# The order of wide and narrow products of two neighbouring weight blocks in a two-layer decoder trunk

## The chip, the core and the metric

The kernel runs on one core of a Trainium2 chip. The metric is the device time of one execution in microseconds (us); the median of three runs of the kernel before is 844.6 us (844.43 to 845.07). A core has several engines that run side by side and wait for one another by semaphores: TensorE (PE in the profile; its weight loads are the row PEld), VectorE (DVE), ScalarE (ACT), GpSimd (POOL) and SyncE (SP, which here only starts transfers).

## The reference

The input x has 256 positions of 2048 features, in float32. Two layers follow one another, each a normalisation, one wide input projection, an attention, a gate, an output projection and a residual addition; a last normalisation ends it.

```python
for i in range(DEPTH):                       # DEPTH = 2
    h = rmsnorm(x, norm_g[i])
    if i % 2 == 0:                           # forgetting attention, 32 heads x 64
        p = h @ fox_w_in[j]                  # q, k, v, gate (2048 each), 32 forget logits
        y = fox_attention(q, k, v, log_f)
        w_out = fox_w_out[j]
    else:                                    # window of 128, 32 query and 4 key heads, sinks, partial rope
        p = h @ swa_w_in[j]                  # q, k, v, gate
        y = swa_attention(q, k, v, swa_sinks[j])
        w_out = swa_w_out[j]
    y = y * silu(gate)
    x = x + y @ w_out
return rmsnorm(x, final_g)
```

Nearly all the arithmetic lies in `h @ w_in` and `y @ w_out`.

## The kernel before, in words

**One product in float32 precision from two halves.** Weights and activations are each split into a high part (rounded to the type fp32r) and a low part (the remainder). ScalarE makes the high half of a weight block (line 210), VectorE the low one (line 211); both lie side by side in a tile `w`. The split activations lie in `xs` (for the input projections) and `ys` (for the output projections). A product needs high times high, high times low and low times high. With `halves` set, the first two are one matmul with a moving operand of 512 columns, whose two halves of 256 columns go to two halves of one PSUM bank: this is called a *wide* product here. The third is a matmul of 256 columns, a *narrow* product. Each matmul is preceded by a load of its stationary operand.

**Units, parts and blocks.** A `Unit` is 256 output features over all 16 slices (`KT`) of the contracted dimension. It is loaded in parts, nearly all of four slices (s = 4). A part is multiplied twice: `block(u, p, 0)` and `block(u, p, 1)` (c = 0 and c = 1) give the two halves of 128 output rows, in two PSUM banks. A block is four wide products and then four narrow ones. After the last part's block, `unit.consume(c, ps)` reads the finished bank: it scales, rotates or splits queries and keys, applies the gate, or adds to the residual. The first unit of layer 1 (`v0`, parts of 1, 2 or 3 slices, 288 columns) and the very last unit have `halves=False`: there all products are 256 or 288 columns wide.

**The order of the work.** `stream` is the list of all parts. The main loop at the end walks over it. For each part it issues the loads of the part three further on (`fetch`), then block c = 0 of this part, then block c = 1 of the part before (`prev`). So a part's weights are used in two steps of the loop. One step is called a *pair* below: two blocks, 16 products. Matmuls keep program order (`mm`, line 73); other instructions are put into order by the framework's planner.

**Ticks.** Each block calls `tick()` after every second product, so four times with s = 4, and eight times a pair. `after(n, fn)` puts work n ticks later. `consume` of c = 0 starts a group's attention: `self.attend(kt, due, ...)` registers scores (PE), transposes (PE), and the product with the values (PE) at fixed numbers of ticks from there. The lists for these ticks are `FOX_DUE`, `FOX_FIRST`, `FOX_LAST`, `SWA_DUE` and `SWA_LAST`:

```python
FOX_DUE = ((16, 34), (40, 60), 106)   # (scores, transposes) of head pairs 0 and 1; values
SWA_DUE = ((16, 40), (44, 64), 74)
```

Between scores and transposes of a pair of heads lies a chain on VectorE and ScalarE: bias and row maximum (line 299), exponentials (line 309), division (line 320). The second normalisation's sums are asked for 10 ticks after the last block of the first layer has been consumed (`after(10, norm)` in `to_layer1`). PSUM is filled with four banks for units (`ps_acc`), two for scores (`ps_s`) and two for transposes and values (`ps_t`). The weight tiles `w` have five buffers.

Of the kernel before, what the change touches and what calls it, by code (L numbers as in the profile page):

```python
# [51 lines left out]
def trunk(  # L52
# [19 lines left out]
    def mm(*args, **kw):  # L72
        tc.keep_in_program_order(nc.tensor.matmul(*args, **kw))  # L73
# [31 lines left out]
    def after(steps, fn):  # L105
        due.setdefault(clock[0] + max(steps, 1), []).append(fn)

    def tick():
        clock[0] += 1
        for fn in due.pop(clock[0], ()):  # L110
            with tc.high_priority(HP):
                fn()
# [103 lines left out]
    def block(unit, p, c):  # L216
        _, _, _, kt0, s = unit.parts[p]
        w, a = loaded[unit, p], unit.acts
        if p == 0:
            pool, tag = unit.acc  # L220
            unit.ps[c] = pool.tile([P, 512], F32, tag=tag, name="acc")
        n = unit.n if unit.kind == "tok" else S
        both, ps = unit.ps[c], unit.ps[c][:, 0:n]
        cs = slice(c * P, (c + 1) * P)
        def operands(i):

            kt = kt0 + i
            if unit.kind == "tok":
                return a[:, kt, 0, cs], a[:, kt, 1, cs], w[:, i]
            return w[:, i, 0, cs], w[:, i, 1, cs], a[:, kt]  # L230

        first, last = kt0 == 0, kt0 + s == KT
        ops = [operands(i) for i in range(s)]
        if unit.halves:

            for i, (sh, _, mv) in enumerate(ops):
                mm(both, sh, mv.rearrange("p h n -> p (h n)"), start=first and i == 0, stop=False)
                if i % 2:
                    tick()
            if s % 2:  # L240
                tick()
            for i, (_, sl, mv) in enumerate(ops):
                mm(ps, sl, mv[:, 0, :], start=False, stop=last and i == s - 1)
                if i % 2:
                    tick()
        else:
            for i, (sh, sl, mv) in enumerate(ops):
                mm(ps, sh, mv[:, 0, :], start=first and i == 0, stop=False)
                mm(ps, sh, mv[:, 1, :], start=False, stop=False)
                mm(ps, sl, mv[:, 0, :], start=False, stop=last and i == s - 1)  # L250
                tick()
        if p == len(unit.parts) - 1:
            unit.consume(c, unit.ps[c])

    def low_half(ps):
        s = work.tile([P, S], F32, tag="row", name="half", bufs=4)
# [292 lines left out]
    def out_units(src, done):  # L549
        def consumer(u):  # L550
            def consume(c, ps):
                m = 2 * u + c
                nc.vector.tensor_add(xT[:, m, :], low_half(ps), xT[:, m, :])
                nc.vector.tensor_add(xT[:, m, :], ps[:, 0:S], xT[:, m, :])
                done(m)

            return consume

        first = [
            Unit(  # L560
                [(src[u, 0], [4, 4]), (src[u, 1][:, 0:4, :], [4]), (src[u, 1][:, 4:8, :], [4])],
                "wgt", consumer(u), acts=ys,
            )
            for u in range(2)
        ]
        return first + [whole(src[u], "wgt", consumer(u), acts=ys) for u in range(2, 8)]
# [195 lines left out]
    last_out = out_units(swa_out_d, to_end)  # L762
# [44 lines left out]
    start = [(u, p) for p in range(3) for u in (v0, q0, k0)]  # L807
# [6 lines left out]
    def fetch(upto):  # L814
        while fetched[0] < min(upto, len(stream)):
            load(*stream[fetched[0]])
            fetched[0] += 1
# [20 lines left out]
    sink = cpool.tile([P, H], F32, name="sink")  # L838
    after(SINK, lambda: nc.gpsimd.dma_start(out=sink, in_=sink_d.partition_broadcast(P)))

    prev = None
    for i, (u, p) in enumerate(stream):
        fetch(i + 1 + LOOK)
        if u is last_out[7]:
            if p == 0:
                block(*prev, 1)
            block(u, p, 0)
            continue
        block(u, p, 0)
        if prev is not None:  # L850
            block(*prev, 1)
        prev = (u, p)
    for p in range(len(last_out[7].parts)):
        block(last_out[7], p, 1)


# ---- launch: one core; the host only lays arrays out
# [62 lines left out]
```

## Time and profile before

| what | value |
|---|---|
| median of three runs | 844.6 us |
| the profiled execution's own time | 844.48 us |
| its span, first to last instruction | 842.7 us |
| PE busy | 830.0 us (98%), 4972 matmuls |
| PE weight loads busy | 720.9 us (86%) |
| VectorE busy | 656.7 us (78%) |
| ScalarE busy | 542.6 us (64%) |
| granted TensorE clock, mean | 0.997 |

The page gives the busy time of each engine, the groups of instructions that cost most, and the chain of work that ended last. A matmul's own duration in these rows (395 ns for 512 columns, 281 to 283 ns for 256) holds its passage through the array, and neighbouring matmuls overlap in it. So what a matmul costs is read from the distance between the starts of two matmuls that follow one another, and an engine that is called busy isn't thereby shown to be at its peak.

### The profile page before, as it was taken

To read this page: it belongs to the slowest core of one execution; us is meant where nothing else is said; L and a number is where in the kernel's file an instruction comes from. 1 tells how busy PE (TensorE), PEld (TensorE's weight loads), DVE (VectorE), ACT (ScalarE), POOL (GpSimd) and SP (SyncE) were. 2 spreads that over 40 slices of the span, in tenths; PEclk is the share of its full clock that TensorE was granted. 3 is DMA by queue.
4 is the path that set the end of the run, shared out by engine and by line. 5 is a ranking of instruction groups with operands and counts; after the bars stand their busy time and mean duration, and the time that the engine had idled before them with its cause. 6 is when DMAs were issued, how large, how long until landed. Compare 5 with 4: busy or idle time off the path is not lost.

```text
span 842.7 us, 13456 instructions
## 1 busy us (share of the span) xinstructions
PE 830.0 (98%) x4972; PEld 720.9 (86%) x4972; DVE 656.7 (78%) x1380; ACT 542.6 (64%) x1061; POOL 67.8 (8%) x93
## 2 busy tenths in 40 slices
PE   8999999999999999999999999999999999999995
PEld 7888888888888888888888888888888888888885
DVE  6898868678686877867677778788898889877555
ACT  7678757667575765746555555567766776666562
POOL 1022001101010010100011110000000000003210
PEclk9999999999999999999999999999999999999998
DMA  8765555555465555554465554544444535364523
GB/s 300 258 218 214 188 187 171 186 192 189 159 227 161 171 209 166 196 177 154 160 211 192 198 195 158 188 159 139 161 150 151 164 137 174 126 203 163 191 100 101
DMA packets 27969, 150.51 MB, mean 179 GB/s; under 512 B 3152, under 2 KB 8176, under 8 KB 12288
## 3 DMA queue, kind: packets, MB, share of 16 engines
q1 hardware_dynamic: 24176, 141.94, 48.9%
q0 software_dynamic: 1408, 6.36, 2.4%
q10 hardware_dynamic: 2320, 1.35, 0.5%
q8 instruction: 39, 0.64, 0.3%
q14 instruction: 26, 0.21, 0.1%
HBM read 147.50 MB, written 2.15 MB: 178 GB/s over the span
## 4 chain that ended last, share of the span: by engine, by line
PE 94%; DVE 4%; ACT 1%; issue 1%; DMA 0%; ACTq 0%; DVEq 0%
PE acc L73 85%; PE ps_s L73 3%; PE psy L73 3%; PE pt L76 2%; DVE w L211 1%; ACT w L210 1%; DMA wraw<-in_vf_dram 0%; DVE st L299 0%; DVE xs L159 0%; DVE xT L667 0%; DVE ssq L784 0%; ACT st L309 0%; DVE q L330 0%; PE ps_n L73 0%; DVE st L320 0%
## 5 line engine op out<-in xcount | busy, mean ns | idle before, releaser
L73 PE MATMUL acc<-xs,w 128*128 128x512 f32 (+1 forms) x2624 | 483.2, 339 | 0.2 <-DVE w L211 0.2
L73 PEld LDWEIGHTS acc<-xs,w 128*128 128x128 f32 x2624 | 405.2, 189 | 59.9 <-issue 3.9
L211 DVE TENSOR_TENSOR w<-wraw,w 128x1024 fp32r<-128x1024 f32 (+3 forms) x271 | 325.1, 1204 | 108.1 <-ACT w L210 106.1
L210 ACT CAST w<-wraw 128x1024 fp32r<-128x1024 f32 (+3 forms) x271 | 277.3, 1028 | 133.3 <-PE acc L73 124.2
L73 PE MATMUL acc<-ys,w 128*128 128x512 f32 x960 | 170.8, 338 | 0.0
L73 PEld LDWEIGHTS acc<-ys,w 128*128 128x128 f32 x960 | 147.4, 189 | 21.5 <-issue 0.6
L73 PE MATMUL acc<-w,xs 128*128 128x256 f32 (+2 forms) x608 | 114.3, 335 | 2.5 <-DVE w L211 1.3
L73 PEld LDWEIGHTS acc<-w,xs 128*128 128x128 f32 x608 | 93.8, 189 | 14.6 <-DVE w L211 2.0
L257 ACT COPY half<-acc 128x256 f32<-128x256 f32 x112 | 41.2, 368 | 60.2 <-PE acc L73 59.3
L309 ACT ACTIVATE st<-st,mx 128x128 f32<-128x128 f32 (+1 forms) x128 | 56.6, 444 | 13.3 <-DVE mx L509 7.9
L576 POOL TENSOR_TENSOR acc<-acc,sq 128x256 f32<-128x256 f32 x28 | 29.9, 1069 | 105.2 <-ACT sq L570 105.2
L363 ACT COPY pts<-pt 128x384 f32<-128x384 f32 x64 | 30.4, 475 | 11.1 <-PE pt L76 11.1
L73 PE MATMUL ps_s<-kk,q 128*128 128x128 f32 (+1 forms) x256 | 35.7, 281 | 0.2
L320 DVE TENSOR_SCALAR st<-st,rl 128x128 f32<-128x128 f32 (+1 forms) x128 | 32.9, 320 | 1.1
L73 PEld LDWEIGHTS ps_s<-kk,q 128*128 128x128 f32 x256 | 32.1, 190 | 1.3 <-issue 0.4
L76 PE MATMUL pt<-ident,st 128*128 128x128 f32 x192 | 31.5, 273 | 0.0
L574 POOL COPY acc<-sq 128x256 f32<-128x256 f32 x2 | 1.9, 936 | 334.0 <-ACT sq L570 334.0
L125 POOL TENSOR_SCALAR_AFFINE_SELECT bc<-bc 128x256 f32<-128x256 f32 x32 | 22.9, 737 | 56.7 <-DMA bc<-negc_d 56.7
L494 POOL DMA_DIRECT2D bc<-negc_d x16 | 8.9, 555 | 214.9 <-DVE mx L508 176.7
L76 PEld LDWEIGHTS pt<-ident,st 128*128 128x128 f32 x192 | 23.2, 140 | 2.3
L159 DVE SCALAR_TENSOR_TENSOR xs<-xT,g_sb,xs 128x256 fp32r<-128x256 f32 x32 | 22.0, 712 | 3.8 <-ACT xs L158 3.8
L329 ACT CAST q<-qT 64x256 fp32r<-64x256 f32 x32 | 12.8, 401 | 18.6 <-DVE qT L697 18.2
(132 smaller groups left out, 578.4 us busy)
## 6 DMA issues: line engine op xcount, KB each, us to landing
wraw<-in_fox_in_dram SPq DMA_DIRECT2D x58, 1024.0 KB, 4.9
wraw<-in_swa_in_dram SPq DMA_DIRECT2D x36, 1024.0 KB, 4.9
wraw<-in_fox_out_dram SPq DMA_DIRECT2D x14, 1024.0 KB, 4.9
wraw<-in_swa_out_dram SPq DMA_DIRECT2D x14, 1024.0 KB, 4.9
bc<-negc_d POOLq DMA_DIRECT2D x16, 384.0 KB, 4.3
wraw<-in_fox_in_dram SPq DMA_DIRECT2D x6, 512.0 KB, 4.5
wraw<-in_fox_out_dram SPq DMA_DIRECT2D x4, 512.0 KB, 3.7
wraw<-in_swa_out_dram SPq DMA_DIRECT2D x4, 512.0 KB, 3.7
```

The source lines that it names most:

```text
L73: tc.keep_in_program_order(nc.tensor.matmul(*args, **kw))
L76: tc.keep_in_program_order(nc.tensor.transpose(out, in_, ident))
L125: nc.gpsimd.affine_select(out=ap, in_=ap, compare_op=ALU.is_ge, fill=NEG, base=base, pattern=pattern, channel_multiplier=mult,)
L159: nc.vector.scalar_tensor_tensor(out=xs[:, kt, 1, :], in0=xT[:, kt, :], scalar=g, in1=xs[:, kt, 0, :].bitcast(F32), op0=ALU.mult, op1=ALU. ...
L210: nc.scalar.copy(w[:, :, 0, :], raw)
L211: nc.vector.tensor_tensor(out=w[:, :, 1, :], in0=raw, in1=w[:, :, 0, :].bitcast(F32), op=ALU.subtract)
L257: nc.scalar.copy(s, ps[:, S : 2 * S])
L309: nc.scalar.activation(st[:, hh, rng], st[:, hh, rng], AF.Exp, bias=nm[:, qb, hh : hh + 1], accum_out=l[:, qb, hh : hh + 1],)
L320: nc.vector.tensor_scalar_mul(st[:, hh, rng], st[:, hh, rng], rl[:, qb, hh : hh + 1])
L329: nc.scalar.copy(q2[w, hh, :], t[w, :])
L363: nc.scalar.copy(group.pts[hh][:, self.j, :], pt[:, 0 : 3 * P])
L576: nc.gpsimd.tensor_add(sums[0], sums[0], s)
```

## The change

`block` no longer issues the narrow products of a block with `halves` itself: it issues the wide ones and returns a function, `narrow`, that issues the narrow ones and then calls `consume` where the part is the unit's last. The main loop calls block c = 0 of the new part (wide products only), then all of block c = 1 of the part before, wide and narrow, and then the new part's narrow products. A block without `halves` is issued whole as before, and what it returns does nothing. In the very last unit the order stays.

The order on PE in one step of the loop was, with four slices: 4 wide (new part, c = 0), 4 narrow (same), 4 wide (part before, c = 1), 4 narrow (same). It becomes: 4 wide (new part), 4 wide (part before), 4 narrow (part before), 4 narrow (new part). The eight ticks of the step move with the products.

```diff
+        def done():
+            if p == len(unit.parts) - 1:
+                unit.consume(c, unit.ps[c])
+
+        def narrow():
+            for i, (_, sl, mv) in enumerate(ops):
+                mm(ps, sl, mv[:, 0, :], start=False, stop=last and i == s - 1)
+                if i % 2:
+                    tick()
+            done()
+
         if unit.halves:
 
             for i, (sh, _, mv) in enumerate(ops):
@@
             if s % 2:
                 tick()
-            for i, (_, sl, mv) in enumerate(ops):
-                mm(ps, sl, mv[:, 0, :], start=False, stop=last and i == s - 1)
-                if i % 2:
-                    tick()
-        else:
-            for i, (sh, sl, mv) in enumerate(ops):
...
-        if p == len(unit.parts) - 1:
-            unit.consume(c, unit.ps[c])
+            return narrow
+        for i, (sh, sl, mv) in enumerate(ops):
...
+        done()
+        return lambda: None
@@
     for i, (u, p) in enumerate(stream):
         fetch(i + 1 + LOOK)
         if u is last_out[7]:
             if p == 0:
-                block(*prev, 1)
-            block(u, p, 0)
+                block(*prev, 1)()
+            block(u, p, 0)()
             continue
-        block(u, p, 0)
+        narrow = block(u, p, 0)
         if prev is not None:
-            block(*prev, 1)
+            block(*prev, 1)()
+        narrow()
         prev = (u, p)
     for p in range(len(last_out[7].parts)):
-        block(last_out[7], p, 1)
+        block(last_out[7], p, 1)()
```

More of the change, by code (lines that the diff above doesn't have):

```diff
@@ L241, in block @@
                 tick()
-            for i, (_, sl, mv) in enumerate(ops):
-                mm(ps, sl, mv[:, 0, :], start=False, stop=last and i == s - 1)
-                if i % 2:
-                    tick()
-        else:
-            for i, (sh, sl, mv) in enumerate(ops):
[L248 to L251, printed above, removed]
-        if p == len(unit.parts) - 1:
-            unit.consume(c, unit.ps[c])
+            return narrow
+        for i, (sh, sl, mv) in enumerate(ops):
+            mm(ps, sh, mv[:, 0, :], start=first and i == 0, stop=False)
+            mm(ps, sh, mv[:, 1, :], start=False, stop=False)
+            mm(ps, sl, mv[:, 0, :], start=False, stop=last and i == s - 1)
+            tick()
+        done()
+        return lambda: None
     def low_half(ps):
```

## The prediction

> **What bounds the kernel now.** I read the head of the page first, then who waited for whom, then the matmuls by form, then single starts in the timeline.
>
> ```profile
> span 842.7 us, 13456 instructions
> ...
> PE 830.0 (98%) x4972; PEld 720.9 (86%) x4972; DVE 656.7 (78%) x1380; ACT 542.6 (64%) x1061; POOL 67.8 (8%) x93
> ...
> PEclk9999999999999999999999999999999999999998
> ```
>
> ```profile
> ACT w L210 <- PE acc L73: 124.2, 110, 2.6
> ...
> PE rows L73 <- DVE tail L655: 2.5, 1, 2.5
> ...
> PE acc L73 <- DVE w L211: 1.4, 3, 0.9
> PE acc L73 <- ACT w L210: 1.1, 2, 0.8
> ```
>
> The second view has total, times and longest, in us. PE waits 2.5 us for weights in all and 2.5 us at the end; ScalarE's weight copies wait 124.2 us for PE to give buffers back. So weights are ahead of PE, and PE's own pace sets the time. The clock is full. A change to the order on PE can act in three ways only: the pace of products, a new wait on PE, or an old wait that goes.
>
> ```profile
> L73 PE MATMUL acc<-xs,w 128*128 128x512 f32 x1312 | 360.7, 395 | 0.0
> L73 PE MATMUL acc<-xs,w 128*128 128x256 f32 x1312 | 212.6, 283 | 0.2 <-DVE w L211 0.2
> L73 PE MATMUL acc<-ys,w 128*128 128x512 f32 x480 | 131.8, 395 | 0.0
> L73 PE MATMUL acc<-ys,w 128*128 128x256 f32 x480 | 76.5, 281 | 0.0
> L73 PE MATMUL acc<-w,xs 128*128 128x512 f32 x256 | 71.0, 399 | 0.0
> L73 PE MATMUL acc<-w,xs 128*128 128x256 f32 x256 | 41.2, 282 | 0.0
> ```
>
> There are 2048 wide and 2048 narrow products (1312 + 480 + 256 of each). Their count, operands and weight loads stay; only where wide meets narrow changes. The 395 and 283 ns overlap from product to product, so the cost has to be read from starts. In the output projection of layer 0, where nothing else is on PE, I asked for moments that lie in one product each; the first figure of a row is its start:
>
> ```profile
> 424.84 0.40 PE L73 MATMUL acc<-ys,w 128*128 128x512 f32 x1
> 425.55 0.39 PE L73 MATMUL acc<-ys,w 128*128 128x512 f32 x1
> 425.77 0.40 PE L73 MATMUL acc<-ys,w 128*128 128x256 f32 x2
> 426.25 0.40 PE L73 MATMUL acc<-ys,w 128*128 128x512 f32 x1
> 426.95 0.40 PE L73 MATMUL acc<-ys,w 128*128 128x512 f32 x1
> 427.18 0.40 PE L73 MATMUL acc<-ys,w 128*128 128x256 f32 x2
> 464.14 0.40 PE L73 MATMUL acc<-ys,w 128*128 128x512 f32 x1
> ```
>
> The rows are the first wide, fourth wide and first narrow product of one block, the same of the next, and the first product 28 blocks after the first row. A block takes (464.14 - 424.84) / 28 = 1.4036 us. Its four wide products take 0.93 us (425.77 - 424.84 and 427.18 - 426.25), about 232 ns each, so its four narrow ones 1.4036 - 0.93 = 0.474 us, 118.5 ns each.
>
> **The pace, which is the term that decides.** The change joins the wide runs of a pair into one of eight, and the narrow runs too. By the stream there are 251 such pairs with parts of four slices (all steps but those that touch `v0` and the last unit; 4 more with smaller parts are left out). Each loses one step from wide to narrow and one back. The trace has no wide run longer than four, but it has a long narrow run in the last unit, two short pairs of runs near the start, and one wide run after scores:
>
> ```profile
> 821.17 5.92 PE L73 MATMUL acc<-w,ys 128*128 128x256 f32 x48
> ...
> 14.67 0.39 PE L73 MATMUL acc<-xs,w 128*128 128x512 f32 x1
> ...
> 16.06 0.40 PE L73 MATMUL acc<-xs,w 128*128 128x512 f32 x1
> ...
> 550.72 0.62 PE L73 MATMUL acc<-xs,w 128*128 128x512 f32 x2
> ...
> 551.63 0.40 PE L73 MATMUL acc<-xs,w 128*128 128x256 f32 x2
> ```
>
> Narrow: 48 products in 5.92 us, the last of which lasts 0.28, are (5.92 - 0.28) / 47 = 120.0 ns each. In a run of four they are 118.5, so a run that follows wide products gets about 6 ns as a gift. A merged run of eight is 474 + 4 x 120.0 = 954 ns against 2 x 474 = 948: +6 ns a pair.
>
> Wide: the gaps between the wide products of a run are (425.55 - 424.84 + 426.95 - 426.25) / 6 = 235 ns, the gap from the last wide one to the narrow one is 0.22 and 0.23, 225 ns. A merged pair has one such last gap less and one inner gap more: +10 ns. The starts are rounded to 10 ns, so I take half, +5.
>
> So I take 11 ns a pair: 251 x 11 = 2.8 us slower. The upper end comes from the short runs: between 14.67 and 16.06 lie two runs of two wide and two narrow, 1.39 us for the eight products that take 1.4036 in runs of four. Halving the number of changes there costs 14 to 15 ns; the same again is 251 x 15 = +3.8 us. The lower end comes from the run after scores: (551.63 - 550.72) / 4 = 227.5 ns each. Should products five to eight of a merged run fall to that from 232.5, a pair gains 20 - 6 = 14 ns: 251 x 14 = -3.5 us. I choose the slower side because the first end has the same kind of step (a boundary more or less) in it, while 227.5 was seen after a break of another kind.
>
> By the Trainium skill, TensorE: Matmul & The Clock Gate, section Back-to-back issue gap, a warm isolated product takes its columns at 2.4 GHz plus about 2.5 ns, so 215.8 and 109.2 ns here, whatever its neighbour; an estimate by that page makes the change worth 0, as in the rival of an even pace below. This trace disagrees with both figures: 232 and 120.0.
>
> **What else moves.** Block c = 0 is finished four narrow and four wide products later than before (1.40 us, four ticks), block c = 1 four narrow ones earlier (0.47 us, two ticks). The weights of the part before come free 0.47 us earlier, which helps transfers and copies that have slack already: nothing. Low weight halves of the new part are needed 1.40 us later, which matters only while PE waits for weights:
>
> ```profile
> 11.29 0.40 PE L73 MATMUL acc<-w,xs 128*128 128x288 f32 x1 [0.75 <-ACT w L210]
> 12.09 0.92 PE L73 MATMUL acc<-w,xs 128*128 128x288 f32 x5 [0.39 <-DVE w L211]
> ...
> 22.73 1.33 PE L73 MATMUL acc<-w,xs 128*128 128x288 f32 x8 [0.88 <-DVE w L211]
> ```
>
> Of these the last ends the lean phase, and it is in `v0`, whose blocks don't change: a wait taken away before 21.6 us comes back there. I cost it at nothing; without that cover at most the 1.4 us of the waits row would be gained.
>
> The norm of layer 1 comes 10 ticks after block c = 1 of the last output unit. Those were two blocks and four wide products, 2 x 1.40 + 0.93 = 3.74 us; now they are four narrow products and two blocks, 0.47 + 2.81 = 3.28: 0.46 less. The last sum on GpSimd, and PE's use of it:
>
> ```profile
> 504.64 0.82 POOL L576 TENSOR_TENSOR acc<-acc,sq 128x256 f32<-128x256 f32 x1 [2.31 <-ACT sq L570]
> ...
> 505.77 0.59 PE L73 MATMUL ps_n<-acc,ones 128*128 128x256 f32 x2
> ```
>
> The sum ends at 505.46, 0.31 us ahead. So PE waits about 0.46 - 0.31 = 0.15 us, once (0 to 1 us, since the work on c = 0 and c = 1 now lies closer together, and everything behind it on PE waits too).
>
> Attention: the ticks between scores and transposes have the same number but other lengths. In layer 0 the first pair of heads has two pairs of blocks and four wide products before and after, the second gets more. In layer 1, second pair of heads (44 to 64), it was two pairs and a block; it becomes two pairs and eight narrow products: 1.40 - 0.95 = 0.45 us less. There the trace has little room:
>
> ```profile
> 712.89 0.98 PEld L73 LDWEIGHTS ps_s<-kk,q 128*128 128x128 f32 x8
> ...
> 714.22 1.23 DVE L211 TENSOR_TENSOR w<-wraw,w 128x1024 fp32r<-128x1024 f32 x1
> ...
> 716.47 0.69 DVE L270 SCALAR_TENSOR_TENSOR gate_e<-gt,gate_e 128x512 f32<-128x512 f32 x1
> ...
> 720.12 1.01 DVE L320 TENSOR_SCALAR st<-st,rl 128x128 f32<-128x128 f32 x4
> ...
> 720.82 0.35 PEld L76 LDWEIGHTS pt<-ident,st 128*128 128x128 f32 x3
> ```
>
> Two of the four divisions (half of 1.01) are needed first, so the transposes have about 0.15 us. The chain itself changes: a weight part (1.23) and a gate step (0.69) stand in it on VectorE now. With c = 1 finished earlier and the scores later, the weight part falls ahead of the scores and leaves. So I take 0, between 0 and 7 groups x (0.45 - 0.15) = 2.1 us.
>
> At the end, block c = 1 of the last unit but one keeps its place, and the last unit isn't changed: 0.
>
> **Sum.** 844.48 + 2.8 + 0.15 = 847.4 us. The profiled execution is 0.12 below the median of the runs, so 847.4 to 847.5 in their terms.
>
> **Rivals.**
> Long wide runs settle (faster). If 227.5 ns is the pace to which a wide run falls when it is long enough, the time is 844.5 - 3.5 = 841.0. For it: the run after 550.72 keeps that pace over four products. Against: the runs of four in the output projection don't reach it, and shorter runs are quicker, not slower. It decides from the fifth product of a run on.
> Even pace (no change). The distances may depend on each product alone and the differences of 10 ns be rounding and bookkeeping of starts; then 844.6. For it: the 28 blocks have one steady 1.4036. Against: 120.0 against 118.5 over 48 products is more than rounding.
> The transposes of layer 1 become the wait (slower still). If the weight part does not leave the chain, PE stands 0.3 us in 7 groups: 847.4 + 2.1 = 849.5. For it: 0.15 us of room against 0.45. Against: the silu of the gate moves ahead by the same shift.
> That matmuls are put back into the old order is excluded, since `mm` keeps program order.
>
> **How the numbers follow.** Forecast 0.40 (846.0 to 848.4), settled wide runs 0.24, even pace 0.24, new waits 0.12. The likeliest is 847.4. The range must reach to the faster case for 8 in 10: 841.0 to 849.6. About 0.2% (1.7 us) can be told from no change, so faster means under 842.9, slower over 846.3. The settled case gives 0.23 faster; the even pace and the low parts of the forecast and of the settled case give 0.30; the rest, 0.47, is slower.
>
> **What would show it.** Right: the narrow products of a run of eight at 118 to 120 ns, the wide ones at 232 to 236 from the second to the seventh, two blocks at 2.82 us against 2.807; PE still without waits in layer 0. The settled case shows as wide products five to eight at 227. A wait of PE for a division (L320) at a transpose would be the fourth case, and one at `ps_n` the small one. Wrong altogether: two blocks at 2.807 us or below.

## The result: 1.8% slower, and where the trace shows it

The changed kernel takes 859.97 us (median of four runs, 858.94 to 860.89) against 844.51 us (844.22 to 845.07) in the same comparison: a ratio of 1.0179, with a 95% interval of 1.0166 to 1.0191. The forecast was 847.4 us with a range of 841.0 to 849.6. The direction was as forecast, though not for the reason given, and the size was not: +15.5 us instead of +2.9.

The head of the page of the changed kernel:

```profile
span 858.2 us, 13466 instructions
...
PE 835.8 (97%) x4972; PEld 724.8 (84%) x4972; DVE 655.0 (76%) x1380; ACT 539.4 (63%) x1061; POOL 80.3 (9%) x93
```

The shares of the chain of work that ended last, in the kernel before:

```profile
PE 94%; DVE 4%; ACT 1%; issue 1%; DMA 0%; ACTq 0%; DVEq 0%
```

and in the changed kernel:

```profile
PE 70%; DVE 15%; ACT 10%; issue 4%; DMA 1%; POOL 0%; DVEq 0%; SPq 0%; ACTq 0%; POOLq 0%
```

So 24 of the chain's 94 per cent of PE have gone, 20 of them to VectorE and ScalarE. The same 4972 matmuls are there. PE's own waits (total, times, longest, in us) are these; in the kernel before there were four rows alone, `rows`, `warm` and the two of `acc` for `w`:

```profile
PE ps_s L73 <- DVE kk L471: 3.3, 7, 0.6
PE rows L73 <- DVE tail L662: 2.5, 1, 2.5
PE ps_n L73 <- POOL acc L583: 2.5, 1, 2.5
PE pt L76 <- DVE st L327: 2.4, 8, 0.4
PE acc L73 <- DVE w L211: 1.7, 3, 1.1
PE warm L73 <- DVE ones L118: 1.1, 1, 1.1
PE acc L73 <- ACT w L210: 0.7, 2, 0.5
PE ps_s L73 <- DVE q L337: 0.5, 1, 0.5
PE ps_s L73 <- DVE mx L306: 0.3, 1, 0.3
```

New are the waits of scores (`ps_s`) for the split keys (`kk`), of the norm (`ps_n`) for the sum on GpSimd, and of transposes (`pt`) for the divided scores (`st`). Their sum is 3.3 + 2.5 + 2.4 = 8.2 us, 9.0 with the two small `ps_s` rows, not 15.5. The view counts idle time from the modelled end of the matmul before, and that end lies behind the point at which a next one could have started: a narrow product lasts 0.28 us in the rows, and the next one starts after 0.12. So I went by starts: for each of the 4972 matmuls the time to the next start, less what a product of that width takes in undisturbed runs of the kernel before, put down to what came next. After less before, in us:

| where | after less before |
|---|---|
| before and between the products of scores | +7.5 |
| before and between transposes | +5.0 |
| before the sums of the norm of layer 1 | +2.7 |
| wide products at half the clock right behind that | +1.6 |
| lean phase at the start and the rest | +0.7 |
| pace of undisturbed products | -2.0 |
| sum (the spans differ by 858.2 - 842.7 = 15.5) | +15.5 |

**The pace became quicker.** The first, fifth wide and first narrow product of a merged pair in the output projection of layer 0, the first of the next pair, and, as the last row, the first product of the pair that comes 21 pairs after the first row:

```profile
446.70 0.40 PE L73 MATMUL acc<-ys,w 128*128 128x512 f32 x1
447.63 0.39 PE L73 MATMUL acc<-ys,w 128*128 128x512 f32 x1
448.54 0.40 PE L73 MATMUL acc<-ys,w 128*128 128x256 f32 x2
449.50 0.40 PE L73 MATMUL acc<-ys,w 128*128 128x512 f32 x1
...
505.36 0.40 PE L73 MATMUL acc<-xs,w 128*128 128x512 f32 x1
```

A pair takes (505.36 - 446.70) / 21 = 2.793 us against 2 x 1.4036 = 2.807: 14 ns less. Wide products one to four take 0.93 us as before, five to eight 0.91, which is 227.5 ns each; the eight narrow ones take the rest, 2.793 - 0.93 - 0.91 = 0.953 us, 119 ns each. By the single starts of these pairs, to the ns, the wide ones of a pair gain about 18 ns and the narrow ones lose about 4; the prediction's lower end had 20 and 6. The faster rival's price, 14 ns a pair, is what was measured. Since scores, transposes and values break many runs, 2.0 us of its 3.5 arrive (by my count 143 pairs run through without a break, and 143 x 14 ns are 2.0 us).

**The norm stops PE and then the clock.** Two stretches of the table of windows, with PE's busy time in the second column and the granted clock behind POOL's:

```profile
510.90:513.60 2.70, 0.21 (x2) 0.01 (x1) 2.67 (x5) 1.63 (x3) 0.72 (x1) 1.00 0.31 130
514.50:517.90 3.40, 3.40 (x10) 2.73 (x10) 2.15 (x5) 0.84 (x2) 0.00 (x0) 0.50 0.70 282
```

PE stands for 2.5 us and then issues the norm's six small products; from 514.5 to 517.9, 3.4 us, the granted clock is at half, and wide products stand 427 ns apart in it. The Trainium skill, TensorE: Matmul & The Clock Gate, Part 1, describes this gate as an activity window of about 3.4 us (3413 ns); the length of the slow stretch agrees. Its section Why this matters for your kernels asks for no gaps over about 3 us; here a wait of 2.5 us was enough, and in a run below (c = 1 consumed at the pair's end) one of 1.6 us.

**Scores wait for keys that stand behind other work.** ScalarE in a middle group of layer 0, in the kernel before:

```profile
231.41 0.37 ACT L257 COPY half<-acc 128x256 f32<-128x256 f32 x1 [0.32 <-PE acc L73]
232.86 1.05 ACT L210 CAST w<-wraw 128x1024 fp32r<-128x1024 f32 x1 [1.08 <-PE acc L73]
233.82 0.40 ACT L460 CAST kk<-k 64x256 fp32r<-64x256 f32 x1
...
235.62 0.37 ACT L257 COPY half<-acc 128x256 f32<-128x256 f32 x1
```

and in the changed kernel:

```profile
234.45 1.05 ACT L210 CAST w<-wraw 128x1024 fp32r<-128x1024 f32 x1 [1.75 <-PE acc L73]
235.40 0.36 ACT L264 COPY half<-acc 128x256 f32<-128x256 f32 x1
237.18 0.37 ACT L264 COPY half<-acc 128x256 f32<-128x256 f32 x1 [1.42 <-PE acc L73]
237.45 1.05 ACT L210 CAST w<-wraw 128x1024 fp32r<-128x1024 f32 x1
238.40 0.41 ACT L467 CAST kk<-k 64x256 fp32r<-64x256 f32 x1
```

`half` is the first step of a block's consumer. Before, the keys of c = 0 went `half` (231.41), one weight copy, `kk` (233.82), all ahead of c = 1 (235.62). After, a weight copy, freed by the block c = 1 of the part before, runs ahead of `half` of c = 0; then `half` of c = 1 and a second weight copy run ahead of the first `kk`. From `half` to the first `kk` it is 3.0 us instead of 2.4, and the eight `kk` steps of c = 0 and c = 1 stand in one queue on ScalarE. On PE the eight score products, with the next product behind them, before and after:

```profile
236.82 1.09 PE L73 MATMUL ps_s<-kk,q 128*128 128x128 f32 x8
237.75 0.63 PE L73 MATMUL acc<-xs,w 128*128 128x512 f32 x2
```

```profile
240.26 0.76 PE L73 MATMUL ps_s<-kk,q 128*128 128x128 f32 x3
241.47 0.86 PE L73 MATMUL ps_s<-kk,q 128*128 128x128 f32 x5 [0.45 <-DVE kk L471]
242.16 0.40 PE L73 MATMUL acc<-xs,w 128*128 128x512 f32 x1
```

They hold PE for 1.90 us instead of 0.93, though the idle time shown is 0.45.

### The profile page after: what moved, and what is told of

Same layout as the page of the kernel before. It is cut to its first block, busy times and chain, and to the rows that moved or that the text cites. A ratio compares the mean times of both kernels' runs of the same rounds, so it can differ in the third digit from the quotient of the medians.

```text
span 858.2 us, 13466 instructions
## 1 busy us (share of the span) xinstructions
PE 835.8 (97%) x4972; PEld 724.8 (84%) x4972; DVE 655.0 (76%) x1380; ACT 539.4 (63%) x1061; POOL 80.3 (9%) x93
## 4 chain that ended last, share of the span: by engine, by line
PE 70%; DVE 15%; ACT 10%; issue 4%; DMA 1%; POOL 0%; DVEq 0%; SPq 0%; ACTq 0%; POOLq 0%
PE acc L73 63%; DVE w L211 5%; ACT st L316 3%; ACT w L210 3%; PE psy L73 2%; PE ps_s L73 2%; PE pt L76 2%; DVE st L327 1%; DVE q L337 1%; ACT kk L467 1%; DVE st L306 1%; DMA xT<-in_xt_dram 1%; DVE gt L289 1%; DVE gt L288 1%; ACT gate_e L275 1%
## 5 line engine op out<-in xcount | busy, mean ns | idle before, releaser
L73 PE MATMUL acc<-ys,w 128*128 128x256 f32 (+1 forms) x960 | 170.9, 338 | 0.2
L73 PE MATMUL acc<-w,xs 128*128 128x512 f32 (+2 forms) x608 | 112.7, 334 | 2.3 <-DVE w L211 1.7
L73 PE MATMUL ps_s<-kk,q 128*128 128x128 f32 (+1 forms) x256 | 38.5, 284 | 4.8 <-DVE kk L471 3.3
L125 POOL TENSOR_SCALAR_AFFINE_SELECT bc<-bc 128x256 f32<-128x256 f32 x32 | 35.7, 1136 | 52.5 <-DMA bc<-negc_d 52.5
L316 ACT ACTIVATION_READ_ACCUMULATOR st<-st,mx 128x1 f32 x128 | 24.0, 187 | 0.0
```

What stands on the lines that cost most here:

```text
L125: nc.gpsimd.affine_select(out=ap, in_=ap, compare_op=ALU.is_ge, fill=NEG, base=base, pattern=pattern, channel_multiplier=mult,)
L316: nc.scalar.activation(st[:, hh, rng], st[:, hh, rng], AF.Exp, bias=nm[:, qb, hh : hh + 1], accum_out=l[:, qb, hh : hh + 1],)
```

## The experiments

Every ratio below is to the kernel before, measured beside it (844.5 to 845.1 us); times are medians.

### The order of before, with a late consumer

```diff
-        block(u, p, 0)
+        done = block(u, p, 0)
         if prev is not None:
-            block(*prev, 1)
+            block(*prev, 1)()
+        done()
...
```

(`block` returns the call of its consumer instead of making it.)

> Order of products as before the change (wide, narrow, wide, narrow), only the consumption of a finished block c = 0 is put off to the end of its pair, 1.4 us later, as the change does. Theory A (the loss comes from consumers and the fixed ticks behind them): c = 0 now finishes its consumer close to c = 1 and just behind a weight copy, so scores of layer 0 wait again about 1 us in each of 6 to 7 groups; the transposes of layer 1 don't wait, because their ticks are as long as before; the norm waits 0 to 2 us. So 849 to 854 us. Theory B (the order of the products itself costs the time): nothing of it is here, so 844.5 within 0.5 us.

Measured: 846.84 us, 1.0025 (1.0016 to 1.0035). The scores didn't wait; the transposes of layer 0 did (`pt`, 1.1 us in PE's waits, 2.4 us by starts). Both theories' times missed, and the edit did less than was meant. In the same group of layer 0 as above:

```profile
232.20 0.37 ACT L260 COPY half<-acc 128x256 f32<-128x256 f32 x1 [0.31 <-PE acc L73]
...
239.02 1.09 PE L73 MATMUL ps_s<-kk,q 128*128 128x128 f32 x8
```

From `half` to the scores it is 6.82 us, where it was 5.41 in the kernel before (231.41 to 236.82). So the planner left the consumer's instructions where c = 0's products end, and only the ticks that are counted from the call came 1.4 us later. Shown is that this delay of the ticks costs 2.2 us; what a late consumer costs by itself, this run doesn't show.

### The norm asked for later

```diff
-            after(10, norm)
+            after(19, norm)
```

> The changed kernel with one number changed: the norm of layer 1 is asked for 19 ticks after the last block instead of 10. Theory A: the 2.7 us that PE stood at the norm's sums go, and with them the 3.4 us of halved clock behind it, which cost 1.6 us: 860.0 - 4.3 = 855.7 us. Rival: the halved clock has another cause, or the wait only moves to the rope factors that need the norm: then 857.3, or 859 to 860.

Measured: 855.96 us, 1.0135 (1.0118 to 1.0152). 4.0 us less than the changed kernel, where 4.3 were expected: the wait is gone, the clock is full up to the end, and the other rows stay (`ps_s` for `kk` 3.3, `pt` 2.5). The wait of 2.5 us thus cost about 1.6 times itself; by starts 1.6 us of that is the halved clock.

### All ticks moved

```diff
-FOX_DUE = ((16, 34), (40, 60), 106)
-FOX_FIRST = ((46, 68), (74, 94), 114)
-FOX_LAST = ((14, 32), (38, 72), 86)
-SWA_DUE = ((16, 40), (44, 64), 74)
-SWA_LAST = ((26, 45), (30, 56), 68)
+FOX_DUE = ((20, 38), (40, 60), 106)
+FOX_FIRST = ((46, 68), (74, 96), 114)
+FOX_LAST = ((20, 36), (38, 72), 86)
+SWA_DUE = ((18, 42), (44, 66), 74)
+SWA_LAST = ((26, 45), (33, 56), 68)
...
-            after(10, norm)
+            after(19, norm)
```

> The changed kernel with its ticks set anew: scores and transposes of layer 0's first pair of heads 4 ticks later (first and last group likewise by 2 to 6), layer 1's scores and transposes 2 ticks later, the norm 9 ticks later. Theory A: the stalls at scores (7.5 us), transposes (5.0) and the norm with its clock (4.3) go, the quicker pace of the merged runs (2.0) stays: 860.0 - 16.8 = 843.2 us, between 842.5 and 844.5. Theory B: what moves is a part of the waits alone, and the merged order stays slower than 844.5, at 848 or over.

Measured: 851.09 us, 1.0076 (1.0061 to 1.0092), 8 us over what theory A gave. Scores and norm no longer wait, but one row of PE's waits grew from 2.4 us to

```profile
PE pt L76 <- DVE st L327: 5.7, 7, 1.0
```

In layer 1 the second pair's transposes were given two ticks more and waited longer (1.0 instead of 0.3 us). That moved ticks change what a chain meets on VectorE is the likely reason; no run here isolates it.

### The narrow products of c = 0 first

```diff
-            block(*prev, 1)()
+        rest = block(*prev, 1) if prev is not None else None
         narrow()
+        if rest is not None:
+            rest()
```

> The changed kernel, but the narrow products of c = 0 go ahead of those of c = 1 (4 wide, 4 wide, 4 narrow of the new part, 4 narrow of the part before); ticks as they were. The runs are as long as in the changed kernel, c = 0 is consumed 0.47 us earlier and c = 1 0.47 us later than there, the weights come free at the end of the pair. Theory A: the norm has its 3.74 us again and waits for little, with the clock full (-4.3), the scores wait less (c = 0 and c = 1 are 3.3 us apart instead of 2.3): 848 to 855 us. Theory B (the merged order): no change, 859 to 861 us.

Measured: 848.46 us, 1.0046 (1.0031 to 1.0061). Runs of eight, ticks untouched, and 11.5 us of the 15.5 are gone: no wait at the norm, none of scores for keys. What is left:

```profile
PE pt L76 <- DVE st L327: 3.9, 5, 0.8
```

at the first transposes of layer 0. So it is not the merged runs that cost the time. Here c = 0 is finished ahead of c = 1 again, and the weights come free at the pair's end. What is left follows from the ticks: the last two of the 18 between these scores and transposes are now four narrow products (0.47 us) and were four wide ones (0.93), so the transposes are asked for 0.46 us earlier.

### Swapped, and two ticks more for those transposes

```diff
-FOX_DUE = ((16, 34), (40, 60), 106)
-FOX_LAST = ((14, 32), (38, 72), 86)
+FOX_DUE = ((16, 36), (40, 60), 106)
+FOX_LAST = ((14, 34), (38, 72), 86)
```

> The kernel with the narrow products of c = 0 ahead of those of c = 1, and one thing more: the first transposes of layer 0 come 2 ticks later (34 to 36, in the last group 32 to 34). Theory A (waits at fixed ticks are all that is lost): the waits at these transposes, 5.9 us in the trace of that kernel, go, no other row waits, and the merged runs keep 2.1 us: 848.5 - 5.5 = 843.0 us, 842.3 to 844.0, so 0.1 to 0.25% faster than the kernel before. Theory B: the waits turn up elsewhere again, as in the kernel with all its ticks moved: 846 or over.

Measured: 843.33 us, 0.9986 (0.9977 to 0.9995): as theory A said, and a little (0.14%) faster than the kernel before.

### The changed kernel, norm and layer 0's ticks

The edit is that of all ticks moved without the two lists of layer 1. (The "956.0 less 100" in the expectation is a slip; 856.0 - 8 is meant.)

> The changed kernel with the norm 9 ticks later and layer 0's ticks moved as in the kernel with all ticks moved, layer 1's ticks left. Theory A: the score stalls of layer 0 (7.5 us) are gone and layer 1's transposes keep the wait of the changed kernel (0.48 us in 7 groups, 3.4 us): 956.0 less 100, that is 856.0 - 8 = 848 us, 847 to 849. Rival (the waits of layer 1 in the kernel with all ticks moved came from layer 0's later work): 850 to 851.

Measured: 849.88 us, 1.0065 (1.0051 to 1.0079), between the two ranges. Scores wait for keys no longer; transposes still do (`pt` 2.8 us in PE's waits: one of 0.9 us in the first group of layer 0, the others in layer 1), and the scores of layer 1's first group wait once for queries (0.5 us in the view, 1.0 by starts).

### And one list entry of layer 1

```diff
-SWA_DUE = ((16, 40), (44, 64), 74)
+SWA_DUE = ((16, 40), (44, 66), 74)
```

> As the one before, and of layer 1 the second transposes alone 2 ticks later (64 to 66), scores and first transposes left. Theory A: the 3.4 us at layer 1's transposes go: 844.5 us, 843.5 to 845.5. Rival (the second pair's chain takes what room it is given, whatever starts it): 848 and over, with the wait at the same transposes.

Measured: 850.51 us, 1.0071 (1.0056 to 1.0086): no gain. Layer 1's transposes no longer wait (the 0.9 us of layer 0's first group stay), and in their place scores of layer 1 wait for queries:

```profile
PE ps_s L73 <- DVE q L337: 1.6, 6, 0.5
```

The rival's time held (848 and over), its place did not: the wait was to stay at the transposes. Here room given at one place is taken at the next. In this order of products I found no list of ticks that comes near the kernel before.

### c = 1 consumed at the pair's end

```diff
+                if late is not None:
+                    late.append(lambda: unit.consume(c, unit.ps[c]))
+                else:
+                    unit.consume(c, unit.ps[c])
...
+            for fn in first:
+                fn()
             done()
...
-            block(*prev, 1)()
-        narrow()
+            block(*prev, 1, late)()
+        narrow(late)
```

> The changed kernel with one thing undone: block c = 1, whose products end before the last four narrow ones of the pair, is consumed only at the end of the pair, as before the change (2.81 us after c = 0 of the same unit instead of 2.34). Products and ticks as in the changed kernel. Theory C (the two consumers lie too close together): the score stalls of layer 0 fall from 7.5 us to under 2, and the norm, which now comes 10 ticks after the pair's end, has 3.74 us again and waits under 0.5: 860.0 - 5.5 - 4.3 = about 850 us. Theory D (tick lengths and the weight copy ahead of c = 0's consumer): the scores stall as before; only the norm's part goes, 855 to 856 us.

Measured: 859.04 us, 1.0169 (1.0155 to 1.0182). The scores stall as in the changed kernel (3.3 us for `kk`), and the norm, asked for 0.46 us later, still waits 1.6, with the granted clock at half behind it from 514.9 to 518.3; by starts the norm costs 0.9 us less, which is what the run is faster by. So the place of the call of c = 1's consumer decides next to nothing. Theory C itself was not tested: only the calls were moved, not the products that feed them, and `half` of c = 1 still starts 1.79 us behind that of c = 0 (235.52 and 237.31), as in the changed kernel (1.78).

### One narrow product of c = 1 put last

```diff
         def narrow():
             for i, (_, sl, mv) in enumerate(ops):
                 mm(ps, sl, mv[:, 0, :], start=False, stop=last and i == s - 1)
                 if i % 2:
                     tick()
+                if split and s == 4 and i == s - 2:
+                    return end
             done()
+            return lambda: None
...
+        def end():
+            mm(ps, ops[-1][1], ops[-1][2][:, 0, :], start=False, stop=last)
+            tick()
+            done()
```

In the loop, block c = 1 issues all but its last narrow product, then come the four of c = 0, then `end`.

> The changed kernel with one product of each pair moved: the last narrow product of c = 1 comes behind the four narrow ones of c = 0. Runs of eight stay; the weights of the part before come free at the end of the pair and no longer 0.47 us ahead of it, and c = 0 finishes just before that instead of after. Ticks as in the changed kernel. Theory E (the weight copies on ScalarE and VectorE start 0.47 us before c = 0 is finished and so run ahead of its consumer): scores of layer 0 no longer wait, the norm waits under 0.5 us with the clock full, and the time falls to the 848 to 851 us of the kernel with all narrow products swapped. Rival (it is c = 0 being 0.93 us later than before, or the tick lengths): c = 0 gains 0.12 us only, so 858 us or more.

Measured: 844.55 us, 0.9995 (0.9986 to 1.0004). One product of 120 ns in each pair, moved by four places, takes away 15.4 us. PE's waits for keys and norm are gone, and ScalarE's order in the same group as above is that of the kernel before again:

```profile
232.92 0.37 ACT L272 COPY half<-acc 128x256 f32<-128x256 f32 x1 [1.58 <-PE acc L73]
233.19 1.05 ACT L210 CAST w<-wraw 128x1024 fp32r<-128x1024 f32 x1
234.25 0.41 ACT L475 CAST kk<-k 64x256 fp32r<-64x256 f32 x1
...
235.84 0.37 ACT L272 COPY half<-acc 128x256 f32<-128x256 f32 x1
```

`half` is ahead of the weight copy, and `kk` follows behind one copy, 1.3 us after `half`. Theory E gave 848 to 851; the gain is larger, since layer 1's transposes lost their wait too. The pace's gain is in this run as well (1.8 us by starts), but smaller waits take it up: 1.0 us once at scores of layer 1 that wait for queries, and 0.2 us in each middle group at layer 0's transposes. What the run does not separate: the weights' release and the end of c = 1 are the same product, so both came 0.47 us later. And the ticks moved with it: c = 0 is now consumed ahead of the pair's last tick, so what is due from it falls one place earlier. For layer 1's second pair of heads that gives 7.9 us from scores to transposes where the changed kernel's ticks gave 7.5, which is at least part of why that wait (3.9 us by starts) is gone.

### Swapped, with three ticks more

```diff
-FOX_DUE = ((16, 34), (40, 60), 106)
-FOX_LAST = ((14, 32), (38, 72), 86)
+FOX_DUE = ((16, 37), (40, 60), 106)
+FOX_LAST = ((14, 35), (38, 72), 86)
```

> The kernel with swapped narrow products and layer 0's first transposes at 36, with one more tick there (37; in the last group 35). In its trace a transpose still waits about 0.14 us in 6 groups. Theory A: this goes, 843.3 - 0.8 = 842.5 us. Rival: the division takes what room it is given, 843.3.

Measured: 842.07 us (841.83 to 842.29), 0.9965 (0.9951 to 0.9978): the fastest kernel of the study. Its PE has no wait left between the lean start and the end but 0.3 us:

```profile
PE rows L73 <- DVE tail L662: 2.5, 1, 2.5
PE acc L73 <- DVE w L211: 1.7, 3, 1.1
PE warm L73 <- DVE ones L118: 1.1, 1, 1.1
PE acc L73 <- ACT w L210: 0.4, 1, 0.4
PE ps_s L73 <- DVE mx L306: 0.3, 1, 0.3
```

### The ticks alone, in the kernel before

The edit is the two lines of 36 and 34 above, in the kernel before.

> The kernel before, with nothing but layer 0's first transposes 2 ticks later (36 and 34), as in the kernel that came out fastest. If that kernel's gain comes from the merged runs, this one stays at 844.6 within 0.3 us; if it comes from the ticks, this one is at 843.3 too.

Measured: 844.52 us, 0.9996 (0.9987 to 1.0005). So these ticks by themselves bring nothing; the gain of the swapped kernel is that of the merged runs.

### Weights asked for one step later

```diff
-LOOK = WBUFS - 2
+LOOK = WBUFS - 3
```

> The changed kernel, products and ticks untouched, with one number changed: weights are asked for one step of the loop later (2 parts ahead of the next instead of 3), so their copies stand one step later in the program, behind the consumer of c = 0 of the step in which their buffer comes free. Theory E (the copy that is released 0.47 us before c = 0 is finished goes ahead of its consumer): with the copy behind it in the program, the scores of layer 0 wait less and the time falls to 846 to 853 us. Rival 1 (c = 1 being finished early is what hurts): no change, 859 to 861. Rival 2 (the planner still puts the copy first because it is ready first): no change either, and the trace shows the copy ahead of the consumer as before.

Measured: 859.20 us, 1.0164 (1.0147 to 1.0181). Rival 2 held: the copy still runs ahead of `half`, and the keys still stand behind c = 1 and a second copy:

```profile
234.87 1.05 ACT L210 CAST w<-wraw 128x1024 fp32r<-128x1024 f32 x1 [1.75 <-PE acc L73]
235.82 0.36 ACT L264 COPY half<-acc 128x256 f32<-128x256 f32 x1
...
238.82 0.41 ACT L467 CAST kk<-k 64x256 fp32r<-64x256 f32 x1
```

So it doesn't decide between the parts that the moved product left together. Open: how much is the copy ahead of c = 0's consumer, how much the earlier end of c = 1, and how much the ticks that moved with them. Shown is that all together, 0.47 us in a pair, are worth 15.4 us.

## Why the prediction was wrong

**The pace (+2.8 us, the term that was said to decide).** The sign was wrong. The step that failed is the choice between the ends: "the first end has the same kind of step (a boundary more or less) in it, while 227.5 was seen after a break of another kind". From the fifth product on a wide run takes 227.5 ns on average with no break before it; the 232 of the short runs was the beginning of a run. The price of the faster rival, 14 ns a pair, was exact; its time (841.0) was not reached in the changed kernel, but the swapped one with its transposes moved shows 842.1. The narrow part (+6 ns a pair, about +4 measured) was about right. So it is luck that the direction came out as forecast: 2.8 of the 2.9 us forecast were this term, and it was a gain of 2.0 us.

**"The weights of the part before come free 0.47 us earlier, which helps transfers and copies that have slack already: nothing."** This step, with the earlier end of c = 1 beside it, cost the forecast: with both put back by 0.47 us, and the ticks that go with them, the time is 844.55 us. That the copies had slack was true (nearly all of PE's waits for weights lie in the lean start); that a copy which starts earlier costs nothing was not. It is 1.05 us on ScalarE and 1.23 on VectorE, it now starts just before c = 0 is finished, and the consumer of c = 0 stands behind it: in the group shown `half` starts about 0.5 us later after the end of c = 0's products than before. The prediction looked at who waits for the copy, not at who queues behind it. How much of the loss is the copy's alone stays open.

**The scores were not priced at all.** The attention step compared the ticks "between scores and transposes" and found layer 0 unchanged. The room ahead of the scores was not looked at. In the kernel before it is small: the last step of the keys' split that the eight score products need ends as the first of them starts.

```profile
236.40 0.42 DVE L464 TENSOR_TENSOR kk<-k,kk 64x256 fp32r<-64x256 f32 x1
```

It ends at 236.82, and the first score product starts at 236.82; the fourth is the one that needs it, 0.29 us later. In the changed kernel the same step ends 1.15 us behind the first product's start (241.41 against 240.26), and the fourth product waits for it. One row of the trace of before would have shown that a delay of keys beyond some 0.3 us is paid. Of the 7.5 us at the scores 6.1 came of it, 0.98 in each of five groups of layer 0 and 1.2 in its last; 1.0 of the rest is one wait of layer 1's first group.

**The norm (0.15 us, bounds 0 to 1).** The mechanism was named and the term mis-sized. The ticks were 0.46 us shorter as computed, but the sum on GpSimd ended 5.9 us after c = 1's last product instead of 3.4, because ScalarE had a weight copy and c = 0's own steps first, and VectorE behind it likewise. The timeline of the changed kernel, from the narrow products behind c = 1's last one to the sum:

```profile
507.68 3.43 PE L73 MATMUL acc<-xs,w 128*128 128x256 f32 x20
507.88 1.05 ACT L210 CAST w<-wraw 128x1024 fp32r<-128x1024 f32 x1 [1.42 <-PE acc L73]
...
509.55 0.35 ACT L264 COPY half<-acc 128x256 f32<-128x256 f32 x1
...
512.85 0.72 POOL L583 TENSOR_TENSOR acc<-acc,sq 128x256 f32<-128x256 f32 x1 [2.07 <-ACT sq L577]
```

c = 1 was done at about 507.7, its `half` ran at 509.55 only (1.9 us later; in the kernel before 0.25), and the sum ends at 512.85 + 0.72 = 513.57. The wait was 2.5 us, and the halved clock behind it, which the prediction didn't have, added 1.6.

**The transposes of layer 1 (chance 0.12, 2.1 us).** It happened as described, with 0.3 us of idle time in 7 groups; by starts it is 3.9 us of the table's 5.0, about 3.1 of them ahead of the first transpose of each group and the rest between the transposes. "the weight part falls ahead of the scores and leaves" was the wrong half of that step: one does, but the next one comes into the middle of the chain.

```profile
732.85 0.16 DVE L747 TENSOR_TENSOR mx<-mx,sink 128x4 f32<-128x4 f32 x1
733.19 1.23 DVE L211 TENSOR_TENSOR w<-wraw,w 128x1024 fp32r<-128x1024 f32 x1 [0.18 <-ACT w L210]
734.33 0.17 DVE L748 TENSOR_SCALAR mx<-mx 128x4 f32<-128x4 f32 x1
```

**The rest held.** The lean start changed by under 1 us, the end of the program not at all, and PE kept program order.

## What to carry to other kernels

When an order on one engine changes, list for each moved end what it frees and what starts then: a copy that has slack itself can still push a consumer that has none. Where ticks or due times were set by hand, measure the room at each of them in the trace of before, ahead of the step as well as behind it, since where the room is a few tenths of a microsecond nearly every delay becomes stall time on the bounding engine. And when an experiment moves a call, look in its trace whether the instructions moved too. The gain that the change was after is there once the finished block and the freed weights come in the old order: the swapped narrow products and two entries of the tick lists gave 842.07 us, 0.35% under the kernel before.

## What the runs showed of the hardware

In the undisturbed pairs of the changed kernel in layer 0's output projection the eight wide products, with a load each, start 233, 236, 228, 233, 231, 227, 227 and 227 ns apart (means over 21 pairs), and the eight narrow ones 113, 119 and six times 120; a pair of eight and eight took 2.793 us against 2.807 for two of four and four. And a single stop of PE of 2.5 us, with six small products behind it, brought the granted clock to half for 3.4 us, so that it cost 4.0 to 4.3 us in all; a stop of 1.6 us at the same place, in another run, did the same to the clock. In the run with all ticks moved, single distances of up to 1.25 us between starts left it full.
